# A hybrid attention block on one core: the mixer's PSUM banks as own tiles in two pools, one weight load set ahead of a reload, filler units placed in other steps

## The chip, the cores and the metric

The kernel runs on one core of a Trainium2 chip. Its engines each have a queue of instructions that they take in order: TensorE (PE, with its weight loads shown apart as PEld), VectorE (DVE), ScalarE (ACT), GpSimd (POOL) and SyncE (SP), which here issues most transfers. The metric is the device time of one execution in microseconds (us). Lower is better.

## What is computed

One layer on h, which is 16 meta tokens followed by 1024 frames of width 1024, all in float32:

```
h = h + 0.5 * swiglu(rmsnorm(h, ffn1_norm), ffn1_w_gate, ffn1_w_up, ffn1_w_down)
u = rmsnorm(h, mix_norm)
aq, ak, av, gq, gk, gv, gr, g_low, gate_a, gate_b = split(u @ w_in)
ya = window_sink_attention(aq, ak, av, att_sinks)          # 8 heads, 2 of keys, window of 3 chunks of 64
log_a = log_sigmoid(g_low @ gla_gate_w + gla_gate_b) / 16
og = gated_linear_attention(gq, gk, gv, log_a)             # S = diag(a) S + k v, o = q S, 4 heads
yb = rmsnorm(og, gla_out_norm) * silu(gr)
mixed = sigmoid(gate_a) * (ya @ w_branch_att) + sigmoid(gate_b) * (yb @ w_branch_gla)
h = h + mixed @ w_out
h = h + 0.5 * swiglu(rmsnorm(h, ffn2_norm), ffn2_w_gate, ffn2_w_up, ffn2_w_down)
return rmsnorm(h, final_norm)[16:]
```

The feed-forward width is 2816.

## The kernel before

**Precision.** Every float32 product is made as three matmuls of rounded operands: high by high, high by low part, low part by high (`mm`, L100 to L105). ACT makes the high part with a copy, DVE the low part with a subtraction (`split` L107, `Weights.cut` L127 for plain weights, `halves` L235 and L236 for the weights called `wop`).

**Order of the work.** FFN1 runs until some 702 us. Its last two feed-forward tiles are done in a loop over two halves of the tokens `c` and eight row blocks `m` (until some 727 us; `pd` is the accumulator there). That loop also starts the normalisation of the mixer's input: `tot` are the token sums of squares of a half, `rep` spreads the scales over rows, and the results are the operands `uh` and `ul`. Then come the projections for keys and queries of the linear attention (`together`, tile `pj`), the low-rank part (`low_rank`), and from 792 to 965 us the *gates stage*: 2048 columns of `w_in` in eight groups, `m` from 0 to 14 in steps of 2. A group is a seven-product scheme for a product of two-by-two blocks: seven products `i` of 12 matmuls of 128x512 each, into three accumulators `pb`, `pa` and `pd`. Product 0, 2, 4 and 6 go to `pb`, 1 to `pa`, 3 and 5 to `pd`. After each product the evacuation `gate_evac` reads the bank: ACT at L1025 copies it to a block `x`, or DVE at L1030 adds it. Weights are made two products ahead (`AHEAD = 2`), and the sums of the next group's weights (`follow.sums`, L443) are made on DVE in the last products of a group. From `m = 8` on generators called `decay` run beside the products: each begins with a matmul into a bank `z` (L1043), which ACT reads at L1044 and DVE at L1045 (writing `b`), and goes on in later products on ACT and DVE. PE, ACT and DVE follow the order of the code in this stage.

After the gates come the projections of attention's keys (AK), values (AV) and first queries (Q0), first one chunk of 512 tokens of each, then the rest (`firsts`). Columns 512 to 1023 of four `uh` and four `ul` tiles were lent to the gates stage and are loaded back from `b12_dram` with 8 loads of 128x512 (L1117), ahead of them. Then attention runs in 16 steps with one list of projection units in each (`slots`): for a step, PE makes the scores of the next one (`sp`), the units, the products with values (`po`, L1331), and the transposes of the next probabilities (`tp`, L1315, of `p`, which DVE writes at L1300). The linear attention (GLA) follows in two passes `p` of eight steps `j`. Sixteen `branch_att` units (`br`, 12 matmuls, weights `w_branch_att`, then a product with a gate `ga` on DVE at L1382, whose gate was loaded at L1378) fill places: one in each of attention's last two steps, four ahead of GLA, four in its pass 0, two in its pass 1, four behind it. GLA's inputs, 12 loads of 128x1024 with two small ones (L1424, L1426), and the gate loads share SP's queue.

**PSUM.** There are eight banks of 512 columns. FFN1 holds them as four tiles of 1024 columns, tags q0 to q3, in one pool. When its last loop ends, `dbl["open"]` is set, and `bank()` hands out the halves of such a double tile one after the other. Who may write a tile is tracked by the scheduler per tile. After the gates stage the pool is closed and a pool of eight single banks is opened (L1121 to L1123).

Of the kernel before, what the change touches and what calls it, by code (L numbers as in the profile page):

```python
# [8 lines left out]
F32 = mybir.dt.float32  # L9
# [6 lines left out]
PSUM = bass.MemoryType.PSUM  # L16

P = 128
# [17 lines left out]
def hybrid_kernel(  # L36
# [4 lines left out]
    nc = tc.nc  # L41
# [4 lines left out]
    psp = ps_singles.enter_context(tc.tile_pool(name="psp", bufs=8, space=PSUM))  # L46
# [3 lines left out]

    dbl, spare = {}, []

    def bank(name="ps"):
        if not dbl.get("open"):
            return psp.tile([P, 512], F32, tag="ps", name=name)
        if not spare:
            both = double(name)
            spare.extend([both[:, 512:], both[:, 0:512]])
        return spare.pop()

# [405 lines left out]
    N1 = T // 2  # L466
# [6 lines left out]
    nc.gpsimd.memset(shift1, 0.0)  # L473
    s_pool = f1.enter_context(tc.tile_pool(name="sums1", bufs=4))

    def acc1(kind, which, turn):

        if dbl["down"]:
            at = 2 * ((turn + (kind != "b")) % 2) + which
        else:  # L480
            at = {"b": 0 if turn % 2 == 0 else 3, "a": 1, "d": 2}[kind]
        return dbl["pool"].tile([P, 1024], F32, tag=f"q{at}", name=f"p{kind}")

# [112 lines left out]
    dgs = {}  # L596
# [162 lines left out]
    ps_singles.close()  # L759
    doubles = ExitStack()  # L760
    dbl.update(down=False, pool=doubles.enter_context(tc.tile_pool(name="psd", bufs=1, space=PSUM)))
    ffn1.gate_ups(range(2, NF - LAST))
# [16 lines left out]
    turns = [0]  # L779

    def double(name):
        turns[0] += 1
        return dbl["pool"].tile([P, 1024], F32, tag=f"q{(turns[0] - 1) % 4}", name=name)

# [39 lines left out]
    dgs = {}  # L824
    sq2 = [x[:, N1:] for x in sqs]

    def add_square(c, m):
        nc.vector.tensor_add(accs[c], accs[c], sqs[m % 3][:, 0:N1] if c == 0 else sq2[m - 1])

    for c in range(2):  # L830
        if c:
            more_sqs = [ffn1.operand(True, "sq2", F32) for _ in range(2)]
            sq2 += [x[:, i * N1:(i + 1) * N1] for x in more_sqs for i in range(2)]
        for m in range(KT):
            acc = Acc(double("pd"), N1)
            n = 0
            for f in range(LAST):
                x, w = mids[LAST * c + f], [y[:, m * P:(m + 1) * P] for y in ws[f]]
# [10 lines left out]
            if c == 0:  # L849
                if m:  # L850
                    add_square(0, m)
                if m in (1, 3):
                    hw[m // 2] = ktiles(wt.cut(raws[m // 2], eng=nc.gpsimd))
            else:
                if m < 2:
                    raws.append(wt.raw(plain_views[2 + m]))
                if m == 2:
                    dgs[0] = scales_of_half(0, double("tot"))
                if m == 4:
                    ps = double("rep")  # L860
                    scales_to_rows(0, (ps, ps[:, 512:]), dgs[0])
                if m > 4:
                    scaled(m - 5, 0)
    dbl["open"] = True

# [11 lines left out]
    b12_dram = dram.tile([4, 2, P, 512], F32, name="b12_dram")  # L877
# [117 lines left out]
    def halves_of(m, c):  # L995
        return u_hi[m][:, c * 512:(c + 1) * 512], u_lo[m][:, c * 512:(c + 1) * 512]
# [117 lines left out]
    manual.__exit__(None, None, None)  # L1114
    for k in range(4):
        for i, x in enumerate(halves_of(k, 1)):
            nc.sync.dma_start(out=x.bitcast(F32), in_=b12_dram[k, i])  # L1117
    g7.close()
    r1.close()
    wt.ws = [w_main]  # L1120
    dbl["open"] = False  # L1121
    doubles.close()
    psp = ctx.enter_context(tc.tile_pool(name="psp", bufs=8, space=PSUM))  # L1123

# [101 lines left out]
    for units in firsts:  # L1226
        units.pop(0)()
    for units in firsts:
        for u in units:
            u()  # L1230
# [161 lines left out]

    slots += [[fill.pop(0)], [fill.pop(0)]]
    values(0)
# [382 lines left out]
```

## Time and profile before

| | us |
|---|---|
| median of three runs | 2059.71 |
| lowest, highest run | 2055.99, 2059.76 |
| the profiled execution, and its span | 2057.24, 2055.5 |
| PE busy | 2006.4 (98% of the span) |
| DVE, ACT, POOL busy | 1403.1, 882.2, 178.4 |
| gates stage with the step out of it, 787 to 966 us: PE busy | 167.16 of 179 |

The page of the profile gives sums for the whole span, and the views behind it (waits, timeline, windows, the chain that ended last) give single instructions. `[2.40 <-DVE b L1045]` behind an instruction means that its engine idled 2.40 us ahead of it, and that the instruction at L1045 that wrote `b` released it. A matmul's row has its whole time through the array, while matmuls that follow each other start closer together than that.

### The profile page before, as it was taken

What the parts mean: (1) busy time and instruction counts of PE and PEld (TensorE: products, weight loads), DVE (VectorE), ACT (ScalarE), POOL (GpSimd) and SP (SyncE); (2) the same over time, 40 slices, a digit from 0 to 9 for tenths busy, and PEclk for the clock granted to TensorE, in tenths of its full rate; (3) what the DMA queues carried; (4) which work ended last, traced back from release to release, by engine and by line L of the source; (5) the groups of instructions that cost most, each with busy time, mean ns of one, the idle gap of its engine ahead of it and who ended that gap; (6) DMA issues with size and microseconds to landing.
All of it is one profiled execution on the core that took longest, in us unless ns stands there. A gap on an engine that the chain in (4) does not pass through costs nothing.

```text
span 2055.5 us, 32054 instructions
## 1 busy us (share of the span) xinstructions
PE 2006.4 (98%) x12084; PEld 1776.6 (86%) x12084; DVE 1403.1 (68%) x2441; ACT 882.2 (43%) x1722; POOL 178.4 (9%) x205
## 2 busy tenths in 40 slices
PE   8899999999999999989999999999999999999998
PEld 7899999999999987777788777888888888878888
DVE  5866677676678785465367658568876866757885
ACT  5534444444322354464256635344544544442222
POOL 1000000001323000002200000120000000022212
PEclk9999999999999999999999999999999999999999
DMA  6333344349975333354312455841543543699822
GB/s 205 106 114 125 125 168 155 125 154 343 359 283 202 101 131 99 103 163 148 79 44 66 164 182 179 262 143 44 183 156 130 179 149 125 206 371 351 278 92 83
DMA packets 285772, 343.06 MB, mean 167 GB/s; under 512 B 26406, under 2 KB 192032, under 8 KB 285616
## 3 DMA queue, kind: packets, MB, share of 16 engines
q1 hardware_dynamic: 267968, 279.60, 41.2%
q10 hardware_dynamic: 17296, 61.29, 8.0%
q8 instruction: 95, 1.56, 0.3%
q14 instruction: 61, 0.50, 0.1%
q0 software_dynamic: 352, 0.11, 0.1%
HBM read 220.66 MB, written 120.27 MB: 166 GB/s over the span
## 4 chain that ended last, share of the span: by engine, by line
PE 86%; DMA 5%; DVE 4%; ACT 3%; issue 1%; SPq 0%; DVEq 0%; ACTq 0%; POOLq 0%
PE pb L460 32%; PE pd L460 17%; PE pa L460 9%; PE pj L103 2%; PE pj L104 2%; PE pj L105 2%; PE wo L103 1%; PE wo L104 1%; PE wo L105 1%; PE br L103 1%; DMA raw<-in_ffn_w_down 1%; PE br L105 1%; PE br L104 1%; PE pd L841 1%; DMA f1mid<-kh 1%
## 5 line engine op out<-in xcount | busy, mean ns | idle before, releaser
L460 PE MATMUL pb<-tt,wop 128*128 128x260 f32 (+1 forms) x2112 | 361.1, 324 | 1.6 <-DVE x L1030 1.6
L460 PEld LDWEIGHTS pb<-tt,wop 128*128 128x128 f32 x2112 | 312.7, 188 | 34.2 <-DVE x L1030 2.4
L236 DVE TENSOR_TENSOR wop<-s,wop 128x512 fp32r<-128x512 f32 x264 | 188.1, 714 | 121.7 <-ACT wop L235 121.2
L235 ACT CAST wop<-s 128x512 fp32r<-128x512 f32 x264 | 163.7, 621 | 236.7 <-PE pb L460 90.0
L460 PE MATMUL pb<-tm,wop 128*128 128x260 f32 (+1 forms) x1440 | 237.5, 321 | 5.9 <-DVE h L347 3.5
L460 PEld LDWEIGHTS pb<-tm,wop 128*128 128x128 f32 x1440 | 209.7, 190 | 26.1 <-DVE h L347 3.9
L235 ACT CAST wop<-raw 128x512 fp32r<-128x512 f32 x198 | 122.9, 621 | 220.5 <-PE pb L460 108.4
L236 DVE TENSOR_TENSOR wop<-raw,wop 128x512 fp32r<-128x512 f32 x198 | 141.1, 715 | 30.7 <-ACT wop L235 30.4
L460 PE MATMUL pd<-tt,wop 128*128 128x260 f32 (+1 forms) x816 | 146.4, 332 | 0.0
L460 PEld LDWEIGHTS pd<-tt,wop 128*128 128x128 f32 x816 | 124.9, 188 | 15.0
L443 POOL TENSOR_TENSOR s<-raw 128x512 f32<-128x512 f32 x28 | 37.6, 1342 | 1057.5 <-DMA tm<-f1mid 453.5
L347 DVE SCALAR_TENSOR_TENSOR h<-pb,h 128x520 f32<-128x520 f32 (+1 forms) x136 | 93.8, 692 | 39.5 <-PE pb L460 37.5
L460 PE MATMUL pd<-tm,wop 128*128 128x260 f32 (+1 forms) x720 | 118.8, 319 | 0.0
L460 PE MATMUL pb<-tb,wop 128*128 128x260 f32 (+1 forms) x672 | 112.3, 320 | 0.5 <-ACT vec L94 0.5
L460 PEld LDWEIGHTS pd<-tm,wop 128*128 128x128 f32 x720 | 104.3, 188 | 9.4
L460 PE MATMUL pd<-tb,wop 128*128 128x260 f32 (+1 forms) x672 | 112.2, 320 | 0.0
L460 PE MATMUL pa<-tb,wop 128*128 128x260 f32 (+1 forms) x672 | 112.0, 320 | 0.0
L460 PEld LDWEIGHTS pb<-tb,wop 128*128 128x128 f32 x672 | 97.9, 188 | 10.0 <-ACT vec L94 0.6
L460 PEld LDWEIGHTS pd<-tb,wop 128*128 128x128 f32 x672 | 97.9, 188 | 9.4
L460 PEld LDWEIGHTS pa<-tb,wop 128*128 128x128 f32 x672 | 97.8, 188 | 9.4
L443 DVE TENSOR_TENSOR s<-raw 128x512 f32<-128x512 f32 x90 | 61.9, 688 | 56.6 <-DMA raw<-in_ffn_w_up 54.9
L103 PE MATMUL pj<-uh,whi 128*128 128x512 f32 (+2 forms) x256 | 93.1, 364 | 5.4 <-ACT whi L132 4.4
(435 smaller groups left out, 4040.6 us busy)
## 6 DMA issues: line engine op xcount, KB each, us to landing
tm<-f1mid ACTq DMA_DIRECT2D x56, 520.0 KB, 6.4
tm<-f2mid ACTq DMA_DIRECT2D x56, 512.0 KB, 5.7
raw<-in_ffn_w_gate SPq DMA_DIRECT2D x42, 512.0 KB, 3.9
raw<-in_ffn_w_up SPq DMA_DIRECT2D x42, 512.0 KB, 4.0
raw<-in_ffn_w_down SPq DMA_DIRECT2D x80, 256.0 KB, 5.5
f1mid<-kh SPq DMA_DIRECT2D x70, 260.0 KB, 3.0
f1mid<-kl SPq DMA_DIRECT2D x70, 260.0 KB, 2.9
f2mid<-kh SPq DMA_DIRECT2D x70, 256.0 KB, 2.8
```

The source lines that it names most:

```text
L103: nc.tensor.matmul(ps, wh[k], xh[k], start=(k == 0), stop=False)
L104: nc.tensor.matmul(ps, wh[k], xl[k], start=False, stop=False)
L105: nc.tensor.matmul(ps, wl[k], xh[k], start=False, stop=(k == n - 1))
L235: nc.scalar.copy(x[:, 0:n], src)
L236: nc.vector.tensor_sub(x[:, n:2 * n], src, x[:, 0:n].bitcast(F32))
L347: nc.vector.scalar_tensor_tensor(hm, ps, 0.5, hm, op0=ALU.mult, op1=ALU.add)
L443: (eng.tensor_add if add else eng.tensor_sub)(a[s], a[x], a[y])
L460: nc.tensor.matmul(ps, y, z[:, s0:s0 + sn], start=(first and k == 0 and at == 0), stop=(at == 2 and k == len(cols) - 1), skip_group_check= ...
L841: nc.tensor.matmul(ps, y, x[:, c0 + s0:c0 + s0 + sn], start=(n == 0), stop=(n == 3 * LAST - 1), skip_group_check=True)
```

## The change

Three edits, with no arithmetic added or left out.

1. **PSUM.** FFN1's four doubles lie in two pools of two. The first is closed in its last loop at `(c, m) = (1, 6)`, the second behind that loop, and each gives way to a pool of four single banks. `bank()` hands out single tiles from then on, two from the one pool and two from the other in turn. The accumulators of the last loop, `tot` and `rep` get fixed places. No pool is closed at the end of the gates stage.
2. **The reload.** The 8 loads from `b12_dram` are issued behind the first unit of AK, AV and Q0, not ahead of them.
3. **Filler units.** Attention's last two steps get two `branch_att` units each, not one. By the loops of GLA, which are as they were, this leaves four ahead of GLA, four in pass 0, none in pass 1, and four behind it.

```diff
     def bank(name="ps"):
-        if not dbl.get("open"):
-            return psp.tile([P, 512], F32, tag="ps", name=name)
-        if not spare:
-            both = double(name)
-            spare.extend([both[:, 512:], both[:, 0:512]])
-        return spare.pop()
+        return psp.tile([P, 512], F32, tag="ps", name=name)
...
+    def two_banks(at, name):
+        return dbl["pools"][at // 2].tile([P, 1024], F32, tag=f"q{at}", name=name)
...
-    doubles = ExitStack()
-    dbl.update(down=False, pool=doubles.enter_context(tc.tile_pool(name="psd", bufs=1, space=PSUM)))
+    dbl.update(down=False, a=ExitStack(), b=ExitStack())
+    dbl["pools"] = [dbl[x].enter_context(tc.tile_pool(name=f"psd{x}", bufs=1, space=PSUM, side=side))
+                    for x, side in (("a", "right"), ("b", "left"))]
...
-    def double(name):
+    def double(name, at=None):
         turns[0] += 1
-        return dbl["pool"].tile([P, 1024], F32, tag=f"q{(turns[0] - 1) % 4}", name=name)
+        return two_banks((turns[0] - 1) % 4 if at is None else at, name)
...
+    PLACES, singles, bank_turn = (0, 1, 2, 3, 0, 1, 2, 3), [], [0]
     for c in range(2):
...
         for m in range(KT):
-            acc = Acc(double("pd"), N1)
+            if (c, m) == (1, 6):
+                dbl["a"].close()
+                singles.append(ctx.enter_context(tc.tile_pool(name="psa", bufs=4, space=PSUM, side="right")))
+            acc = Acc(double("pd", m % 4 if c == 0 else PLACES[m]), N1)
...
                 if m == 2:
-                    dgs[0] = scales_of_half(0, double("tot"))
+                    dgs[0] = scales_of_half(0, double("tot", 2))
                 if m == 4:
-                    ps = double("rep")
+                    ps = double("rep", 3)
...
-    dbl["open"] = True
+    dbl["b"].close()
+    singles.append(ctx.enter_context(tc.tile_pool(name="psb", bufs=4, space=PSUM)))
+
+    def bank(name="ps"):
+        bank_turn[0] += 1
+        return singles[(bank_turn[0] - 1) // 2 % 2].tile([P, 512], F32, tag="ps", name=name)
...
-    for k in range(4):
-        for i, x in enumerate(halves_of(k, 1)):
-            nc.sync.dma_start(out=x.bitcast(F32), in_=b12_dram[k, i])
     g7.close()
     r1.close()
     wt.ws = [w_main]
-    dbl["open"] = False
-    doubles.close()
-    psp = ctx.enter_context(tc.tile_pool(name="psp", bufs=8, space=PSUM))
...
     for units in firsts:
         units.pop(0)()
+    for k in range(4):
+        for i, x in enumerate(halves_of(k, 1)):
+            nc.sync.dma_start(out=x.bitcast(F32), in_=b12_dram[k, i])
     for units in firsts:
...
-    slots += [[fill.pop(0)], [fill.pop(0)]]
+    slots += [[fill.pop(0), fill.pop(0)] for _ in range(2)]
```

**PE in the gates stage**, where product 0 of group `m = 10` ends (`pb`), the two matmuls into `z` stand, and product 1 begins. Before (each name is that of the double tile, given by whoever took its first half):

```order
L460 MATMUL pb<-uh_8387,wop 128x512
L460 MATMUL pb<-ul_8395,wop 128x512
L460 MATMUL pb<-uh_8387,wop 128x512
L1043 MATMUL pb<-glow,gw 128x512 [waits Activation_49]
L1043 MATMUL z<-glow,gw 128x16
L460 MATMUL z<-uh_8388,wop 128x512 [waits DVE_49]
L460 MATMUL z<-ul_8396,wop 128x512
```

and in the changed kernel, where L453 is the L460 of before, L1051 its L1043, and uh_8391 its uh_8388:

```order
L453 MATMUL pb<-uh_8390,wop 128x512
L453 MATMUL pb<-ul_8398,wop 128x512
L453 MATMUL pb<-uh_8390,wop 128x512
L1051 MATMUL z<-glow,gw 128x512
L1051 MATMUL z<-glow,gw 128x16
L453 MATMUL pa<-uh_8391,wop 128x512 [waits Activation_49]
L453 MATMUL pa<-ul_8399,wop 128x512
L453 MATMUL pa<-uh_8391,wop 128x512 [waits DVE_49]
```

`[waits ...]` names the engines, or the queues of transfers, whose signal an instruction waits for. The order is the same. The first `z` matmul waits for nothing, and product 1 waits with its first matmul for ACT alone (its weights' high part) and with its third for DVE (their low part), where it waited for DVE ahead of all.

**SP behind the gates stage.** Q0's weights are two loads `raw<-in_w_in 128x8x64`. Before:

```order
L124 DMA raw<-in_w_in 128x8x64 [waits DMAHW5_49,DVE_49]
L1117 DMA uh_8384<-b_dram 128x512 [waits DMAHW6_49,PE_49]
...
L1073 DMA km_dram<-k 128x512 [waits DMAHW5_49,DVE_49]
L1117 DMA ul_8392<-b_dram 128x512 [waits DMAHW6_49]
...
L1117 DMA ul_8395<-b_dram 128x512 [waits DMAHW4_49]
L124 DMA raw<-in_w_in 128x8x64 [waits DMAHW5_49]
```

and in the changed kernel:

```order
L117 DMA raw<-in_w_in 128x8x64 [waits DMAHW5_49,DVE_49]
L117 DMA raw<-in_w_in 128x8x64 [waits DMAHW6_49]
L1027 DMA gates<-x 128x512 [waits DMAHW7_49,DVE_49]
...
L1081 DMA km_dram<-k 128x512 [waits DMAHW5_49,DVE_49]
L1232 DMA uh_8387<-b_dram 128x512 [waits DMAHW6_49,PE_49]
...
L1232 DMA ul_8398<-b_dram 128x512 [waits DMAHW5_49]
```

Q0's second load passes seven stores and the eight reloads, and the first reload passes the seven stores to the other side.

**DVE in attention's last two steps**, from the maxima of the last scores to the low parts `ptl` that step 14's or 15's `po` matmuls read. Before:

```order
L1295 TENSOR_SCALAR mx<-mx 128x4 [waits DVE_49]
L1382 TENSOR_TENSOR ga<-br,ga 128x512 [waits DMAHW6_49,DMAHW7_49,DMAHW4_49,PE_49]
L1298 RECIPROCAL sm<-sm 128x4 [waits Activation_49]
L1300 TENSOR_SCALAR p<-p,sm 128x210 [waits DVE_49]
L1300 TENSOR_SCALAR p<-p,sm 128x210 x3
L1341 TENSOR_TENSOR u<-po,qs_10599 64x256 [waits PE_49,Activation_49]
L1341 TENSOR_TENSOR u<-po,qs_10599 64x256
L109 TENSOR_TENSOR ptl<-tp,pth 82x512 [waits Activation_49]
```

and in the changed kernel:

```order
L1300 TENSOR_SCALAR mx<-mx 128x4 [waits DVE_49]
L1387 TENSOR_TENSOR ga<-br,ga 128x512 [waits DMAHW6_49,DMAHW7_49,DMAHW4_49,PE_49]
L1303 RECIPROCAL sm<-sm 128x4 [waits Activation_49]
L1305 TENSOR_SCALAR p<-p,sm 128x210 [waits DVE_49]
L1305 TENSOR_SCALAR p<-p,sm 128x210 x3
L1387 TENSOR_TENSOR ga<-br,ga 128x512 [waits DMAHW5_49,DMAHW7_49,DMAHW0_49,PE_49]
L1346 TENSOR_TENSOR u<-po,qs_10622 64x256 [waits DMAHW3_49,DMAHW5_49,PE_49,Activation_49]
L1346 TENSOR_TENSOR u<-po,qs_10622 64x256
L102 TENSOR_TENSOR ptl<-tp,pth 82x512 [waits Activation_49]
```

A second product with a gate stands ahead of `u` and `ptl`, and it waits for a load.

## Rows read from the trace of the kernel before

**Rows 1.** From the page: the span, and busy time of each engine with its share of the span.

```profile
span 2055.5 us, 32054 instructions
PE 2006.4 (98%) x12084; PEld 1776.6 (86%) x12084; DVE 1403.1 (68%) x2441; ACT 882.2 (43%) x1722; POOL 178.4 (9%) x205
```

**Rows 2.** The waits of PE over the whole span: who waited for whom, us in total, how often, the longest.

```profile
PE pj L103 <- ACT whi L132: 4.4, 1, 4.4
PE z L460 <- DVE b L1045: 4.1, 2, 2.4
...
PE tp L1315 <- DVE p L1300: 3.5, 3, 2.7
...
PE z L1043 <- DVE b L1045: 2.5, 1, 2.5
...
PE pb L460 <- DVE x L1030: 1.6, 2, 0.8
PE pb L460 <- ACT x L1025: 1.4, 2, 0.7
PE pb L1043 <- ACT x L1025: 1.4, 2, 0.7
...
PE pj L103 <- DVE x L1030: 1.0, 1, 1.0
...
PE pj L924 <- ACT sums L806: 0.5, 1, 0.5
```

**Rows 3.** The timeline of PE in the gates stage: start, us, instruction, and in brackets the idle time ahead of it with its releaser. The first row is product 1 of group 0, the second product 1 of group 12.

```profile
797.75 0.50 PE L460 MATMUL pb<-uh,wop 128*128 128x512 f32 x1 [0.68 <-ACT x L1025]
...
922.81 0.73 PE L460 MATMUL z<-uh,wop 128*128 128x512 f32 x1 [2.40 <-DVE b L1045]
```

**Rows 4.** The chain that ended last, in the gates stage: start, us, what. Each row is one product of 12 matmuls.

```profile
903.50 2.73 PE pb L460 x12
...
922.81 4.61 PE z L460 x12
...
946.74 4.44 PE pa L460 x12
```

**Rows 5.** The timeline of DVE ahead of the second row of Rows 3.

```profile
917.08 0.68 DVE L236 TENSOR_TENSOR wop<-raw,wop 128x512 fp32r<-128x512 f32 x1
...
921.41 0.68 DVE L236 TENSOR_TENSOR wop<-s,wop 128x512 fp32r<-128x512 f32 x1
922.01 0.74 DVE L1045 TENSOR_SCALAR b<-z,vec 128x512 f32<-128x512 f32 x1
```

**Rows 6.** Windows: stretch, its length, busy time (and instructions) of PE, PEld, DVE, ACT and POOL, the mean clock granted to PE, the busy share of the DMA engines, and GB/s. The first row is the gates stage.

```profile
787.00:966.00 179.00, 167.16 (x721) 132.88 (x720) 96.47 (x166) 93.41 (x160) 4.22 (x12) 0.98 0.39 120
...
910.00:920.00 10.00, 9.93 (x44) 7.91 (x43) 9.69 (x22) 6.35 (x11) 0.00 (x0) 1.00 0.52 165
920.00:930.00 10.00, 7.60 (x26) 5.75 (x25) 4.65 (x8) 2.72 (x5) 0.00 (x0) 0.83 0.56 182
...
980.00:990.00 10.00, 8.32 (x28) 6.96 (x29) 1.57 (x1) 1.05 (x1) 8.78 (x20) 0.66 0.41 82
```

**Rows 7.** The timeline of SP's queue of transfers behind the gates stage. The rows at L124 are Q0's two loads (the second begins a run of three issues), the row at L1073 the last of the stores, the row at L1117 the last reload.

```profile
963.96 0.38 SPq L124 DMA_DIRECT2D raw<-in_w_in  x1
...
969.79 0.40 SPq L1073 DMA_DIRECT2D km_dram<-k  x1
...
973.34 0.42 SPq L1117 DMA_DIRECT2D ul<-b_dram  x1
973.81 5.27 SPq L124 DMA_DIRECT2D raw<-in_w_in  x3
```

**Rows 8.** The chain that ended last, behind the gates stage: Q0's second load, and single matmuls of Q0's first unit, the first one behind the wait, the last but one at the slower rate, and one behind it. Between the first two, eleven matmuls of 512 columns and seven of 256 stand in all.

```profile
973.81 6.74 DMA raw<-in_w_in
...
981.67 0.79 PE pj L103
...
987.38 0.43 PE pj L103
...
988.54 0.23 PE pj L104
```

**Rows 9.** The view of transfers: what, by which queue, how often, KB each, median us from issue to landing.

```profile
uh<-b_dram SPq DMA_DIRECT2D x4, 256.0 KB, 4.7
```

**Rows 10.** The timeline of DVE in attention's last steps, products with a gate (`ga`, idle time ahead in brackets).

```profile
1174.13 0.69 DVE L1382 TENSOR_TENSOR ga<-br,ga 128x512 f32<-128x512 f32 x1
...
1190.08 1.29 DVE L1382 TENSOR_TENSOR ga<-br,ga 128x512 f32<-128x512 f32 x2 [5.62 <-DMA ga<-gates]
```

**Rows 11.** Windows, with the columns of Rows 6, of attention's last steps.

```profile
1160.00:1170.00 10.00, 10.00 (x63) 8.53 (x62) 6.40 (x21) 6.62 (x19) 0.00 (x0) 1.00 0.72 237
...
1181.00:1192.00 11.00, 11.00 (x52) 9.17 (x51) 2.99 (x6) 1.47 (x4) 1.16 (x7) 1.00 0.83 263
```

**Rows 12.** Windows, with the columns of Rows 6, of GLA's pass 1.

```profile
1220.00:1230.00 10.00, 10.00 (x71) 7.30 (x71) 7.58 (x21) 4.08 (x15) 0.00 (x0) 1.00 0.51 170
1230.00:1240.00 10.00, 10.00 (x74) 7.17 (x72) 6.98 (x21) 6.33 (x18) 0.00 (x0) 1.00 0.23 79
1240.00:1247.00 7.00, 6.59 (x52) 4.67 (x49) 5.70 (x19) 3.80 (x19) 0.00 (x0) 1.00 0.33 112
```

**Rows 13.** Windows, with the columns of Rows 6, of the start of the mixer's projections.

```profile
727.00:740.00 13.00, 12.94 (x58) 10.18 (x57) 13.00 (x27) 7.54 (x18) 0.00 (x0) 1.00 0.18 59
```

More of the change, by code (lines that the diff above doesn't have):

```diff
@@ L49, in hybrid_kernel @@
     r_main = ctx.enter_context(tc.tile_pool(name="rmain", bufs=2))
-    dbl, spare = {}, []
     def bank(name="ps"):
-        if not dbl.get("open"):
-            return psp.tile([P, 512], F32, tag="ps", name=name)
-        if not spare:
-            both = double(name)
-            spare.extend([both[:, 512:], both[:, 0:512]])
-        return spare.pop()
+        return psp.tile([P, 512], F32, tag="ps", name=name)
     TP = 1088
@@ L474, in hybrid_kernel @@
     s_pool = f1.enter_context(tc.tile_pool(name="sums1", bufs=4))
+    dbl = {}
+    def two_banks(at, name):
+        return dbl["pools"][at // 2].tile([P, 1024], F32, tag=f"q{at}", name=name)
     def acc1(kind, which, turn):
@@ L481, in acc1 @@
             at = {"b": 0 if turn % 2 == 0 else 3, "a": 1, "d": 2}[kind]
-        return dbl["pool"].tile([P, 1024], F32, tag=f"q{at}", name=f"p{kind}")
+        return two_banks(at, f"p{kind}")
     ffn1 = Seven("f1", N1, acc1, (t_a, t_b, blk, s_pool, w_ext), ffn1_w_gate, ffn1_w_up, ffn1_w_down)
```

## The prediction, made before the changed kernel ran

> **What bounds the kernel now.** I read the page first: PE is busy 2006.4 us of a span of 2055.5, so nearly all of the time is matmuls that the change leaves as they are, and DVE with 68% has room on average [rows 1]. What can be won is PE's idle time, 49.1 us, and stretches in which its clock is low. So the list of PE's waits came next, to see which of them the edits touch: waits in the gates stage for `b` (L1045) and `x` (L1025, L1030), one for Q0's weights, one for `tp`, one for `sums` [rows 2]. The stage windows then show where the idle time sits: PE is busy 167.16 of 179 us in the gates stage, while DVE has only 96.47 there [rows 6]. A stage in which no engine is full and PE still stands waits for order, not for throughput.
>
> The timeline says which order. Product 1 of group 0 goes to `pa`, and waits 0.68 us for the ACT copy of product 0, which is in `pb` [rows 3]. Nothing computed by that copy enters product 1. The two accumulators are halves of one double tile, and the wait is the tile's, not the bank's. It is worst where a `z` shares a double tile with an accumulator: product 1 of group 12 waits 2.40 us for `b` [rows 3], and `b` is late since DVE did the next group's sums and other steps between 917.08 and 922.01, in a window in which it was busy 9.69 of 10 us [rows 5, 6].
>
> **The gates stage.** With own tiles these waits have no object: the order of the changed kernel gives `z` no wait and product 1 its two weight waits alone. Removed are 4.1 + 2.5 us for `b`, 1.6 + 1.4 for `x` ahead of products, and 1.4 for `x` ahead of `z` [rows 2]: 11.0 by rounded rows, and 10.8 by the unrounded waits that they sum. I take 10.8.
>
> A second term is the clock. Behind the two longest waits a product of 12 matmuls takes 4.61 and 4.44 us, where 2.73 is usual [rows 4], and the granted clock is 0.83 in the window of the first [rows 6]. That is a stretch at the lower of the two levels, 1.2 GHz in place of 2.4. It goes with the waits: (4.61 - 2.73) + (4.44 - 2.73) = 3.6 us. The page "TensorE: Matmul & The Clock Gate" of the Trainium skill (section on why this matters for your kernels) warns only of idle gaps longer than either of these two. By it the 3.6 us would have another cause and stay, and the forecast would stand 3.6 us higher; the rows show the low clock right behind 2.40 us of idling, and the rows decide.
>
> What is late next? The weights. PE then asks for product 1's weights at some 920.4 in place of 922.81. They were made on DVE by 917.76; those of product 2 are made by 922.1, ahead of the `b` that no longer matters to PE [rows 5], and product 2 would start at about 923.1. The slack is 1.0 us there, so the feed can cost between 0 and the whole of the three long waits and their clock (rival A). I take 0.4 us. Term: **-14.0**.
>
> **Out of the gates.** Closing the pool costs 1.0 us: AK's first matmul waits for the last `x` [rows 2]. Single tiles that stay open need no close, so it goes. Then Q0: its first load is issued at 963.96, its second at 973.81, behind the eight reloads and the stores between them, and lands 6.74 us later [rows 7, 8]. PE idles 4.4 us for its high part [rows 2], and then runs at the lower level: a matmul of 128x512 takes 0.43 us at 987.38 and 0.23 at 988.54, with a clock of 0.66 in the window [rows 8, 6]. From 981.67 to 987.8 it ran so, 6.1 us of which half is lost, 3.0. In the change both loads are issued at about 964.4 and land, by the same 6.74, near 971. PE reaches Q0 two units behind the stage's end at 965, each of 24 matmuls x 0.23 = 5.5 us: at 976. The waits and the low clock go: 1.0 + 4.4 + 3.0 = **-8.4**.
>
> The eight reloads are moved past these units in the program, but in SP's queue seven of the eight stood behind the stores already, of which the last was issued at 969.79; the last reload went at 973.34 [rows 7]. A reload lands 4.7 us after issue [rows 9], so at about 978; the second chunks need them from 965 + 3 x 5.5 = 981.5. The cover is 3.5 us, and if it fails, rival B follows. I count it at nothing.
>
> **Attention's end.** The second unit in step 14 puts 12 matmuls, 2.7 us, between the scores of step 15 and its `tp`, which waited 2.7 us for `p` [rows 2]. That wait is filled: **-2.4**, a few tenths left. The second unit's product with a gate stands on DVE ahead of `u` and `ptl`. Such products waited for their loads between nothing and 5.62 us, at 1190.08 [rows 10], while PE idled none of it [rows 11]. Now `po` of step 15 is queued behind `ptl`; two units of 2.7 us on PE cover it. Between 0 and 5.6, nearest to the row at 1174.13 that did not wait: **+0.5**.
>
> **GLA.** Pass 1 loses two units of 2.7 us. DVE's work in it is 7.58 + 6.98 + 5.70 = 20.3 us [rows 12], units' evacuations included, against 27 - 5.4 = 21.6 us of PE work left: DVE nearly level. The part of the pass without units lost 7.00 - 6.59 = 0.4 us in 7 [rows 12]; over 21.6 us that is 1.3. Bounds 0 and 5.4 (the whole cover): **+1.5**.
>
> **The mixer's start.** `tot` now stands one block of the last FFN1 loop later: 12 matmuls of 260 columns, 2.73 x 260 / 512 = 1.4 us. DVE is busy 13.00 of 13 us just behind, where PE takes its `ul` one by one [rows 13], so part of the delay shows at the end: between 0 and 1.4, **+1.0** since DVE has no slack. The wait for `sums`, where `rep` shared a double tile with `pj`, goes: **-0.5** [rows 2].
>
> Sum: -14.0 - 8.4 - 2.4 + 0.5 + 1.5 + 1.0 - 0.5 = **-22.3**. The profiled execution took 2057.24, which gives 2034.9. The median of the three runs, 2059.71, is 2.5 above that execution, and from it the sum is 2037.4. I forecast 2036, between the two.
>
> **The rivals.**
> A. *The weights take the place of the banks.* In groups 10 to 14 PE still waits behind DVE, now for `wop`. For it: 9.69 of 10 us busy on DVE [rows 6] and a slack of one microsecond. Against it: the order `wop`, then `b` [rows 5], and a mean of 96.47 in 179. Price: the three waits, 2.5 + 4.1, and the clock, 3.6: 10.2, so 2046.
>
> B. *The reloads come late.* Each waits for PE in the order, which might mean the end of the first three units, not of the last gates product. PE would then stand at the second chunks as it stood at Q0, 4.4 + 3.0, so 2043. Against it: AK's first unit ran in the kernel before ahead of the reloads' landing though it stood behind them in the program, so parts of these tiles are tracked apart.
>
> C. *DVE is held by a gate load, and the kernel is slower than before.* In steps 14 and 15 the gate loads share SP's queue with GLA's 12 inputs of 128x1024, 6.3 MB. If a gate that DVE waits for ahead of `ptl` lands behind all of them, at 237 GB/s [rows 11] that is 26.5 us, and then 3.0 of low clock as at Q0: 29.5, so 2065. It makes the kernel slower once some 28 us of it are exposed, nearly all of the queue. Against it: 5.62 us is the longest such wait, with PE busy 11.00 of 11 [rows 10, 11].
>
> D. *The change does not do what it says*: the single tiles are taken in an order that brings the same waits back, within 0.2% of 2059.7. Against it: the rows of the order. The page "PSUM — Partial Sum Buffer" of the Trainium skill (on bank collisions) asks for guarding by bank and quarter of the partitions, by which a neighbouring bank needs no wait; the trace shows one of 0.68 us between two banks, so it came from the tile.
>
> **How the numbers follow.** Forecast 0.72, A 0.10, B 0.08, C 0.05, D 0.05. The low end is the sum with its losses at their lower bounds, -22.3 - 0.4 - 0.5 - 1.5 - 1.0 = -25.7, from the profiled execution 2031.5, less 3 for other small waits and the scatter of runs: 2028. The high end takes in A and B: 2047. Outside are C and D. Some 0.2% is what a measurement of this kernel can tell from no change. Faster: forecast, A and B, 0.90; same: D, 0.05; slower: C, 0.05.
>
> **What would show it.** In the gates stage, no wait of PE for `b` or `x`, all products at 2.7 us, and PE busy beyond 0.98 of the stage. No wait for Q0's `whi`, and a clock near 1 behind the stage. `tp` of step 15 waiting under 0.5 us. Some 1 to 2 us of new waits in GLA's pass 1 for `attb` or `st`, and about 1 near 730 us. Wrong would be: waits for `wop` of 1 us and more in groups 10 to 14, a wait at the second chunks for a reload, or a stall of PE at `po` of step 15.

## The result, and the profile after

| | before | changed |
|---|---|---|
| median, us | 2057.85 (4 runs) | 2032.48 (4 runs) |
| lowest, highest | 2054.92, 2059.76 | 2029.48, 2035.58 |
| ratio of the runs | | 0.9878, 95% interval 0.9856 to 0.9901 |
| profiled execution, span | 2057.24, 2055.5 | 2034.17, 2032.5 |

The change takes 25.4 us off the median and 23.0 off the profiled span; the sum said 22.3. The page of the changed kernel answers to [rows 1]: 23 us less of span, and 7.4 less of busy time for the same matmuls, in part since the clock was lower for less of the time (mean granted clock 0.992 before, 0.995 now).

```profile
span 2032.5 us, 32056 instructions
...
PE 1999.0 (98%) x12084; PEld 1776.5 (87%) x12084; DVE 1400.4 (69%) x2441; ACT 882.1 (43%) x1722; POOL 178.2 (9%) x205
```

The waits of PE over the whole span (who waits for whom, us in total, times, the longest) answer to [rows 2]. Every wait there for `b`, `x`, `whi` and `sums` is gone, and the longest for `p` too. The list of the changed kernel has new, shorter ones: for `qs`, `o` and `ga`. The first row is FFN1's.

```profile
PE pg L631 <- ACT a L648: 7.1, 1, 7.1
...
PE br L96 <- ACT qs L1342: 1.2, 1, 1.2
...
PE tp L1320 <- DVE p L1305: 0.8, 2, 0.6
...
PE br L97 <- DVE qs L1347: 0.7, 1, 0.7
PE ot L1528 <- DVE o L1516: 0.7, 1, 0.7
PE go L1493 <- DVE ga L1387: 0.5, 1, 0.5
...
PE go L1493 <- DVE attb L1487: 0.5, 1, 0.5
```

The windows, with the columns of [rows 6], show the gates stage and what is now the first part of the projections behind it: PE busy 178.86 of 179 us at a clock of 1.00.

```profile
787.00:966.00 179.00, 178.86 (x804) 146.26 (x803) 102.90 (x176) 97.06 (x165) 16.27 (x41) 1.00 0.48 149
```

SP's timeline answers to [rows 7]. Both loads for Q0 are issued in a row at 950.41 (x2), and the eight reloads follow from 956.30 to 959.79.

```profile
950.41 1.01 SPq L117 DMA_DIRECT2D raw<-in_w_in  x2
956.30 0.45 SPq L1232 DMA_DIRECT2D uh<-b_dram  x1
...
959.79 0.42 SPq L1232 DMA_DIRECT2D ul<-b_dram  x1
```

To see where 23 us went I cut both profiles at the first matmuls of certain tiles. The view of one tile gives them, here `pj` in the changed kernel: times of one matmul, then first and last start.

```profile
L96 PE MATMUL pj<-uh,whi x256: 278/389/501, 951.5 to 1144.3; 128*128 128x512 f32 x80, 128*128 128x256 f32 x24, 128*128 128x272 f32 x24
...
L953 PE MATMUL pj<-uh,w x24: 276/287/398, 789.6 to 796.8; 128*32 128x512 f32 x8, 128*32 128x256 f32 x8, 128*32 128x272 f32 x8
```

So the gates stage with the low-rank part runs from 789.6 to 951.5, 161.9 us. The stretches of all profiles, in us:

| kernel | FFN1 to the last loop | that loop | projections | low-rank, gates | AK to first scores | attention | first filler unit to `wo` | `wo` | FFN2 |
|---|---|---|---|---|---|---|---|---|---|
| before | 702.4 | 24.9 | 58.9 | 180.0 | 63.1 | 140.8 | 133.5 | 88.4 | 663.5 |
| before, second profile | 702.2 | 24.9 | 59.0 | 179.9 | 61.6 | 140.8 | 135.0 | 88.5 | 663.3 |
| changed | 705.8 | 26.2 | 57.6 | 161.9 | 55.5 | 140.7 | 135.2 | 88.4 | 661.2 |
| changed, second profile | 702.4 | 26.1 | 57.6 | 161.9 | 55.6 | 140.6 | 134.8 | 88.4 | 660.9 |
| banks_alone | 701.5 | 26.1 | 57.6 | 161.9 | 57.3 | 140.7 | 135.0 | 88.4 | 661.5 |
| reload_first | 706.4 | 26.1 | 57.6 | 161.9 | 57.3 | 140.7 | 135.0 | 88.5 | 661.8 |
| one_unit_per_step | 702.1 | 26.1 | 57.7 | 161.8 | 55.6 | 140.7 | 135.7 | 88.5 | 661.3 |
| old_banks_reload_late | 704.6 | 24.9 | 58.9 | 181.3 | 55.6 | 140.7 | 133.4 | 88.4 | 661.3 |
| sums_early | 702.5 | 24.9 | 58.9 | 180.5 | 61.8 | 140.7 | 134.0 | 88.4 | 661.7 |
| two_then_one | 705.3 | 26.2 | 57.6 | 161.9 | 55.5 | 140.7 | 133.5 | 88.5 | 661.2 |
| two_ahead_of_gla | 702.6 | 26.1 | 57.7 | 161.9 | 55.5 | 140.8 | 133.1 | 88.4 | 662.0 |
| first_half_units | 703.1 | 26.1 | 57.6 | 161.9 | 55.5 | 140.7 | 134.2 | 88.4 | 661.4 |
| fillers_mended | 703.2 | 26.2 | 57.6 | 161.9 | 55.6 | 140.7 | 134.9 | 88.5 | 661.4 |
| closed_together | 701.9 | 26.1 | 57.6 | 162.0 | 55.5 | 140.7 | 139.5 | 88.5 | 661.1 |

Stretches that an edit does not touch mostly repeat to 0.2 us from kernel to kernel, and tell apart what runs that scatter by 5 us can't. FFN1, whose order of work no edit changes, scatters between 701.5 and 706.4: 705.8 and 702.4 are one and the same kernel. Where PE waits, the second profile of the kernel before differs from the first by 1.5 us in two stretches, so a difference from the kernel before is given by both.

### The profile page after: what moved, and what is told of

Same layout as the page of the kernel before. It is cut to its first block, busy times and chain, and to the rows that moved or that the text cites. A ratio compares the mean times of both kernels' runs of the same rounds, so it can differ in the third digit from the quotient of the medians.

```text
span 2032.5 us, 32056 instructions
## 1 busy us (share of the span) xinstructions
PE 1999.0 (98%) x12084; PEld 1776.5 (87%) x12084; DVE 1400.4 (69%) x2441; ACT 882.1 (43%) x1722; POOL 178.2 (9%) x205
## 5 line engine op out<-in xcount | busy, mean ns | idle before, releaser
L453 PE MATMUL pb<-tt,wop 128*128 128x260 f32 (+1 forms) x2208 | 383.9, 327 | 0.0
L453 PEld LDWEIGHTS pb<-tt,wop 128*128 128x128 f32 x2208 | 330.9, 188 | 35.5
L453 PE MATMUL pb<-tm,wop 128*128 128x260 f32 (+1 forms) x1440 | 235.9, 320 | 5.5 <-DVE h L340 3.3
L453 PEld LDWEIGHTS pb<-tm,wop 128*128 128x128 f32 x1440 | 208.6, 190 | 25.1 <-DVE h L340 3.7
L453 PE MATMUL pd<-tt,wop 128*128 128x260 f32 (+1 forms) x768 | 135.1, 329 | 0.0
L453 PEld LDWEIGHTS pd<-tt,wop 128*128 128x128 f32 x768 | 115.9, 188 | 13.1
L453 PE MATMUL pd<-tm,wop 128*128 128x260 f32 (+1 forms) x720 | 118.8, 319 | 0.0
L453 PE MATMUL pb<-tb,wop 128*128 128x260 f32 (+1 forms) x672 | 112.3, 320 | 0.5 <-ACT vec L87 0.5
L453 PEld LDWEIGHTS pd<-tm,wop 128*128 128x128 f32 x720 | 104.3, 188 | 9.3
L453 PE MATMUL pd<-tb,wop 128*128 128x260 f32 (+1 forms) x672 | 112.2, 320 | 0.0
L453 PE MATMUL pa<-tb,wop 128*128 128x260 f32 (+1 forms) x672 | 112.0, 320 | 0.0
L453 PEld LDWEIGHTS pb<-tb,wop 128*128 128x128 f32 x672 | 97.9, 188 | 9.9 <-ACT vec L87 0.6
L453 PEld LDWEIGHTS pd<-tb,wop 128*128 128x128 f32 x672 | 97.9, 188 | 9.3
L453 PEld LDWEIGHTS pa<-tb,wop 128*128 128x128 f32 x672 | 97.8, 188 | 9.3
L340 DVE SCALAR_TENSOR_TENSOR h<-pd,h 128x520 f32<-128x520 f32 (+3 forms) x112 | 72.7, 655 | 33.3 <-PE pd L453 17.5
```

What stands on the lines that cost most here:

```text
L340: nc.vector.scalar_tensor_tensor(hm, ps, 0.5, hm, op0=ALU.mult, op1=ALU.add)
L453: nc.tensor.matmul(ps, y, z[:, s0:s0 + sn], start=(first and k == 0 and at == 0), stop=(at == 2 and k == len(cols) - 1), skip_group_check= ...
```

## Experiments: the three edits apart

**The changed kernel again**, beside the next three on one chip.

> The changed kernel once more, as the reference for the three partial kernels that run beside it on the same chip. Theory 1 (own tiles in the gates stage and the order of Q0's loads carry the gain, the filler units carry none of it): 1.2% below the kernel before, some 2033 us beside 2058. From the start of the low-rank part to AK's first matmul some 162 us beside 180, from there to the first scores 55.5 beside 63.1, from the first filler unit to the first w_out matmul 135.2 beside 133.5. Rival (part of the gain is scatter of FFN1 and FFN2, whose code is the same): the gain shrinks to some 20 us or less.

2032.75 us, ratio 0.9881 (0.9867 to 0.9895). The gain is not scatter.

**The third edit undone.**

```diff
-    slots += [[fill.pop(0), fill.pop(0)] for _ in range(2)]
+    slots += [[fill.pop(0)], [fill.pop(0)]]
```

> The changed kernel with the third edit undone: one filler unit in each of attention's last two steps, so two in GLA's pass 1 again. Theory 1 (the filler units fill the wait of 2.7 us for p, but bring waits for the last attention output, for gate loads and in pass 1 that cost more): 1 to 2 us faster than the changed kernel, some 2031; from the first filler unit to the first w_out matmul 133.5 us, the wait of tp back at 2.7 us, the waits for qs gone, and those of pass 1 near 0.4. Rival (the prediction's sum: filler units gain 0.4 on balance): 0.4 us slower than the changed kernel.

2030.83 us, ratio 0.987 (0.9857 to 0.9884), inside the changed kernel's interval. The stretch took 135.7 us where I expected 133.5: wrong. The wait for `p` is back at its old length, in PE's timeline:

```profile
1150.64 1.56 PE L1320 MATMUL tp<-ident,p 128*82 128x128 f32 x8 [2.69 <-DVE p L1305]
```

But here a low clock came behind it, which the window of this kernel shows (mean clock 0.86), and the first profile of the kernel before did not have:

```profile
1144.00:1154.00 10.00, 7.31 (x35) 6.09 (x34) 7.94 (x25) 5.53 (x17) 0.00 (x0) 0.86 1.01 357
```

So the stretch of the kernel before is 133.5 or, with the low clock, 135.0, as in its second profile. Beside that, the third edit changes the stretch by between -0.9 and +1.7 us, by which profile it is held against. In sum it can't be told from nothing.

**The second edit undone.**

```diff
+    for k in range(4):
+        for i, x in enumerate(halves_of(k, 1)):
+            nc.sync.dma_start(out=x.bitcast(F32), in_=b12_dram[k, i])
     g7.close()
...
     for units in firsts:
         units.pop(0)()
-    for k in range(4):
-        for i, x in enumerate(halves_of(k, 1)):
-            nc.sync.dma_start(out=x.bitcast(F32), in_=b12_dram[k, i])
```

> The changed kernel with the second edit undone: the eight reloads from b12_dram ahead of the first units. Theory 1 (Q0's second load stands behind the stores and reloads in SP's queue): PE waits 4 to 5 us for Q0's whi again and runs at the lower clock behind it, AK's first matmul to the first scores 63 us, some 7 us slower than the changed kernel, 2040. Rival (the wait came from the pool that was closed, not from the queue): no wait, same time as the changed kernel.

2038.35 us, ratio 0.9913 (0.9896 to 0.9929). The median is 5.6 us above the changed kernel, near what I expected, but not for my reason. AK to the first scores took 57.3 us, 1.8 longer and not 7.5, and PE has no wait for `whi`. The rest of the difference to `changed_again`'s profile lies in FFN1 (706.4 beside 702.4) and FFN2 (661.8 beside 660.9), where the order of work is the same. `banks_alone` below, with the same order of loads but one filler unit per step, has the lower median again. So 1.8 us is what the second edit is worth beside the new banks, by the stretch; why this kernel's four runs lay higher is open.

**The second edit alone, on the kernel before.**

```diff
-    for k in range(4):
-        for i, x in enumerate(halves_of(k, 1)):
-            nc.sync.dma_start(out=x.bitcast(F32), in_=b12_dram[k, i])
     g7.close()
...
     for units in firsts:
         units.pop(0)()
+    for k in range(4):
+        for i, x in enumerate(halves_of(k, 1)):
+            nc.sync.dma_start(out=x.bitcast(F32), in_=b12_dram[k, i])
```

> The kernel before with the second edit alone: reloads behind the first units, banks as halves of double tiles, one filler unit per step. Theory 1 (edits add up): some 7.5 us faster than the kernel before, 2050; the gates stage as in the kernel before, with the waits for b and x and the low clock behind two of them. Rival (with the old banks the pool's close holds the queue as well, so that the order of loads alone gains little): under 3 us faster.

2050.85 us, ratio 0.9972 (0.996 to 0.9984). As expected: 55.6 us from AK to the first scores, 7.5 less than in the first profile of the kernel before and 6.0 less than in the second, and the waits for `b` and `x` as before. The order of Q0's loads is worth 6.0 to 7.5 us beside the old banks and 1.8 beside the new.

**The first edit alone**, formed from that difference (both edits above undone in the changed kernel).

> The first edit alone: own banks in two pools, with the reloads ahead of the first units and one filler unit per step. Theory 2 (formed from the runs so far: with the banks free the scheduler itself puts second chunks of AK and AV ahead of Q0's first unit, and the late load costs 2 us in place of 7.5): gates stage 161.9 us, AK to the first scores 57.3, first filler unit to w_out 133.5 to 135.7, about 2034, so that the banks carry 22 or more of the 24.5 us. Theory 1 in its first form (the edits' parts add up as in the prediction, 14 and 8): AK to the first scores 63, about 2040.

2032.58 us, ratio 0.9874 (0.9857 to 0.9892): the banks alone give all of the gain that the medians can tell; the stretches leave 1.8 us to the second edit. Theory 2 stands, my first theory's sum of parts falls. Q0's `whi` is as late as ever in this kernel, cast on ACT behind a wait of 5.98 us for the load:

```profile
961.86 1.05 ACT L125 CAST whi<-raw 128x1024 fp32r<-128x1024 f32 x1 [5.98 <-DMA raw<-in_w_in]
```

but PE is not at Q0 then. The scheduler put AK's last chunk (24 matmuls of 128x272) ahead of Q0's first unit, and PE waits only for single reloads in it:

```profile
959.21 0.39 PE L97 MATMUL pj<-ul,whi 128*128 128x272 f32 x1 [0.16 <-DMA ul<-b_dram]
...
960.67 0.39 PE L97 MATMUL pj<-ul,whi 128*128 128x272 f32 x1 [0.40 <-DMA ul<-b_dram]
```

The order of PE's units (tile, weights, columns, matmuls) says the same. Before:

```
pj_10766 whi_10762 128x512 2 | pj_10795 whi_10692 128x256 7 | pj_10766 wlo_10763 128x512 22
```

where whi_10762 is Q0's, taken up behind AK's and AV's first units. With own banks and the old order of loads, whi_10793 being Q0's:

```
pj_10857 whi_10723 128x272 24 | pj_10894 whi_10760 128x256 3 | pj_10797 whi_10793 128x512 2
```

**When the first pool is closed.**

```diff
-            if (c, m) == (1, 6):
-                dbl["a"].close()
-                singles.append(ctx.enter_context(tc.tile_pool(name="psa", bufs=4, space=PSUM, side="right")))
...
+    dbl["a"].close()
+    singles.append(ctx.enter_context(tc.tile_pool(name="psa", bufs=4, space=PSUM, side="right")))
     dbl["b"].close()
```

> The changed kernel with the first pool of doubles closed behind the last FFN1 loop, with the second, and not two row blocks ahead of its end. Theory (the gain is from the banks being own tiles, not from the time of the close; the four banks of the first pool are read long before the first projection): the stretch from the loop to the low-rank part 83.8 us as in the changed kernel, within half a us, gates stage 161.9, time the same. Rival (the early close is what lets PE run into the projections without a wait, and the tile tracking then holds PE for the last pd): 1 us or more of waits of PE near 730 us and a longer time by as much.

2034.28 us, ratio 0.9882 (0.9866 to 0.9899): the same, and the same 26.1, 57.6 and 162.0 us in the stretches that it touches. The early close of the first pool is not what gains. That there are two pools was not tried apart.

## Experiments: the waits and the clock behind them

**The sums one product earlier in DVE's queue**, on the kernel before.

```diff
-                if j == 8:
+                if j == 7:
                     follow.sums(nc.vector)
```

> The kernel before with one line moved: the four sums of the next group's weights stand one product earlier in DVE's queue, so ahead of the product whose bank shares a tile with z by one product more. No bank and no work changes. Theory 1 (the long waits for b are DVE's queue ahead of b, and the low clock is caused by the length of these waits): the two waits of 2.4 us for b shrink to about 0.8, the clock stays at 1 in the gates stage, and the stage from the low-rank part to AK loses 2 x 1.6 + 3.6, some 7 us of its 180; the waits of 0.7 and 0.8 us for x stay. Rival (DVE is short of throughput in these groups): the waits move to another product or to the weights, and the stage gains under 2 us.

2058.49 us, ratio 1.0001 (0.9991 to 1.0012): no gain, and the rival was nearer. PE's waits from 780 to 1035 us in this kernel:

```profile
PE pj L103 <- ACT whi L132: 4.2, 1, 4.2
PE z L460 <- DVE b L1045: 3.5, 2, 1.8
PE pd L460 <- ACT wop L235: 2.4, 2, 1.2
PE z L1043 <- DVE b L1045: 1.8, 1, 1.8
PE pb L460 <- ACT x L1025: 1.7, 2, 1.0
...
PE pd L460 <- DVE x L1030: 0.9, 2, 0.5
```

The waits for `b` shrank to 1.8 us and not to 0.8, since DVE, now ready earlier, waits ahead of `b` for ACT's reading of the same `z`:

```profile
925.02 0.75 DVE L1045 TENSOR_SCALAR b<-z,vec 128x512 f32<-128x512 f32 x1 [0.67 <-ACT e L1044]
```

and new waits came for weights (2.4) and for a late evacuation (0.9). The clock stayed at 1.00 from 880 to 970 us, and the product behind the wait took 3.01 us, not 4.61:

```profile
925.83 3.01 PE z L460 x12
```

So the low clock is a cost of its own, which can go without the wait. The stage took 180.5 us all the same: the new waits took what the clock gave back. This order on DVE does not remove the waits; other orders were not tried.

**The kernel before, a second profile.**

> The kernel before once more, for a second profile of it. Theory (the low clock behind waits of 1.7 to 2.7 us comes behind some of them and not others, from run to run): the same waits as in the first profile to a tenth of a us, but other products among those behind them take 4 us and more, and the gates stage differs from 180.0 by a us or two. Rival (the low clock is fixed by the length of the wait): the same two products as in the first profile.

The chain of this profile has the low clock behind the same two waits, at 922.64 and 946.55, within 0.2 us of the times in [rows 4], and 3.01 us behind a wait of 1.7:

```profile
900.31 3.01 PE z L460 x12
...
922.64 4.61 PE z L460 x12
...
946.55 4.44 PE pa L460 x12
```

That speaks for the rival. But in `old_banks_reload_late`, where this stage begins 2.2 us later and the waits are as long, the chain reads otherwise:

```profile
902.68 5.49 PE z L460 x12
...
927.93 4.31 PE z L460 x12
...
951.88 2.84 PE pa L460 x12
```

The low clock came behind the wait of 1.7 us, and not behind one of 2.45. So neither stands: the length of a wait alone does not decide, and yet the two profiles of one kernel, 0.2 us apart in this stage, have it behind the same waits. The wait for `p` (2.69 to 2.70 us in all three) had no low clock behind it in the first profile, and a clock of 0.83 in the second:

```profile
1170.00:1180.00 10.00, 7.31 (x34) 5.87 (x33) 6.80 (x23) 4.34 (x14) 0.00 (x0) 0.83 0.96 369
```

Q0's wait differs too: 4.0 us with a clock of 0.83 behind it, beside 4.4 and 0.66 in the first profile [rows 2, 6], and AK to the first scores took 61.6 us beside 63.1:

```profile
980.00:990.00 10.00, 8.83 (x38) 7.55 (x39) 1.24 (x2) 1.63 (x2) 8.81 (x21) 0.83 0.38 73
```

## Experiments: the filler units

In the changed kernel, DVE's timeline behind attention shows what the second units brought. Two products with a gate wait 4.08 and 0.72 us for their loads, ahead of `u` and the last `qs`:

```profile
1162.57 0.69 DVE L1387 TENSOR_TENSOR ga<-br,ga 128x512 f32<-128x512 f32 x1 [4.08 <-DMA ga<-gates]
1163.98 0.69 DVE L1387 TENSOR_TENSOR ga<-br,ga 128x512 f32<-128x512 f32 x1 [0.72 <-DMA ga<-gates]
```

and PE waits for `qs`, since the next units are those on tokens 512 to 1023:

```profile
1163.49 1.20 PE L96 MATMUL br<-qs,whi 128*128 128x512 f32 x4 [1.22 <-ACT qs L1342]
1166.26 0.50 PE L97 MATMUL br<-qs,whi 128*128 128x512 f32 x1 [0.70 <-DVE qs L1347]
```

In pass 1 DVE is nearly full (9.03 of 10) and PE waits for it:

```profile
1210.00:1220.00 10.00, 8.84 (x72) 6.51 (x74) 9.03 (x26) 4.79 (x16) 0.00 (x0) 1.00 0.16 52
```

**One unit given back.**

```diff
-    slots += [[fill.pop(0), fill.pop(0)] for _ in range(2)]
+    slots += [[fill.pop(0), fill.pop(0)], [fill.pop(0)]]
```

> The changed kernel with two filler units in attention's step 14 and one in step 15; one unit comes back to GLA's pass 1. Theory 1 (the second unit of step 14 fills the wait for p; what costs are the waits for qs and the missing units in pass 1): the wait of tp stays near nothing and some of the loss goes: from the first filler unit to the first w_out matmul 133.5 us or less, 1 to 2 us faster than the changed kernel. Rival (any unit taken from GLA is lost there): as the changed kernel, 135.

2033.52 us, ratio 0.9878 (0.9864 to 0.9893); the stretch 133.5 us, 1.3 to 1.7 less than in the changed kernel. As expected by the stretch; the median doesn't show it.

**Two units ahead of GLA, two in pass 1.**

```diff
-    for _ in range(4):
+    for _ in range(2):
         fill.pop(0)()
     for p in range(2):
```

> The changed kernel with two filler units ahead of GLA in place of four, so that pass 1 has its two again. Theory 1: the waits of pass 1 (o, attb, 1.5 us) go, those for qs and the gate (1.9 and 0.5) stay, since the first unit behind attention still needs its last output: 133.5 to 134.5 us in that stretch. Rival (the loss is all in the waits for qs): 135 as in the changed kernel.

2029.94 us, ratio 0.986 (0.9845 to 0.9875), the stretch 133.1 us. The waits of pass 1 went, one of those for `qs` stayed:

```profile
PE br L96 <- ACT qs L1342: 1.2, 1, 1.2
PE go L1493 <- DVE a L1529: 0.8, 1, 0.8
...
```

From the first filler unit to the first `br` product that reads GLA's output it took 88.6 us, beside 90.5 in the changed kernel. Not all of these 1.9 us are pass 1's. From the first state product of pass 1 to that `br` product it is 32.1 us in the changed kernel, and 36.3 here with two more units of 2.72: 1.2 us are what the units missing in pass 1 cost. The other 0.7 lie ahead of it, where the second wait for `qs` (0.7) and the one for a gate (0.5) are gone as well.

**Units on the first half of the tokens first.**

```diff
-    fill = fill[0][0:2] + fill[1][0:2] + fill[0][2:4] + fill[1][2:4] + fill[2] + fill[3]
+    fill = fill[0][0:2] + fill[1][0:2] + fill[2][0:2] + fill[0][2:4] + fill[1][2:4] + fill[2][2:4] + fill[3]
```

> The changed kernel with the filler units in another order: the third set's two units on tokens 0 to 511 come ahead of all units on tokens 512 to 1023, so that the first two behind attention don't read its last output. Theory 1 (PE waits there for qs, which DVE writes behind two products that wait for gate loads): the waits for qs, 1.9 us, go, the waits of DVE for gate loads stay and cost PE nothing there; pass 1 as in the changed kernel: 133 us in that stretch. Rival (GLA's inputs, not qs, hold PE there): 135.

2029.4 us, ratio 0.9861 (0.9845 to 0.9876), the stretch 134.2 us. The waits for `qs` went as expected, and PE then idled 2.6 us at GLA's first state, until 1174.40:

```profile
PE kv L1478 <- issue: 2.6, 1, 2.6
```

The profile names no releaser, but DVE's timeline shows one that fits. That product reads `km`, which DVE copies at L1464, behind products with a gate that wait for their loads, and the copy ends 0.1 us ahead of it:

```profile
1171.78 1.31 DVE L1387 TENSOR_TENSOR ga<-br,ga 128x512 f32<-128x512 f32 x2 [0.61 <-DMA ga<-gates]
1173.42 0.69 DVE L1387 TENSOR_TENSOR ga<-br,ga 128x512 f32<-128x512 f32 x1 [0.33 <-DMA ga<-gates]
1174.03 0.27 DVE L1464 COPY km<-km 16x128 f32<-16x128 f32 x1
```

So the expectation that DVE's waits for gate loads cost PE nothing here was wrong, and GLA's inputs, the rival's cause, are not what shows: its other operand, `gvm`, shows its last landing at 1170.2 (one of its four loads shows none).

**Both together.**

> The changed kernel with both changes of the filler units together: two of them ahead of GLA in place of four, and the units on the first half of the tokens first. Theory (the missing units of pass 1 cost 1.9 us, the waits behind attention 2.2): from the first filler unit to the first w_out matmul 131 to 132.5 us beside 135, about 2029 and the fastest kernel of the study. Rival (the waits behind attention are for GLA's inputs, which PE meets as soon as the waits for qs are gone): 133, as with either change alone.

2031.64 us, ratio 0.9867 (0.9852 to 0.9882), the stretch 134.9 us, beside 131 to 132.5 and 133 expected: neither number came, but the rival's mechanism did. PE waits at the same product, now for one of GLA's small inputs, which SP issues behind the twelve large ones:

```profile
1169.10 0.54 PE L1478 MATMUL kv<-gvm,km 16*64 16x128 f32 x4 [2.49 <-DMA gvm<-gvm_dram]
```

With two units ahead of GLA and no wait for `qs`, PE reaches it before its inputs have landed. The low clock came behind this wait (mean clock 0.66 from 1169 to 1174 us), and the unit behind it took 4.54 us, 1.7 more than at the full clock; without that the stretch would be near the rival's 133. Behind the 2.58 us in `first_half_units` it did not come (1.00 from 1172 to 1182). The fastest medians of the study, 2029.4 and 2029.9, are 2.5 to 3.1 us below the changed kernel's, inside its interval.

In `closed_together` the gate loads came later still. A step of GLA waits 2.87 us for DVE, held by such a product, and the clock fell to 0.78 in the window; both make its stretch 139.5:

```profile
1182.12 0.79 PE L1492 MATMUL go<-gv,attb 128*128 128x128 f32 x2 [2.87 <-DVE ga L1386]
```

```profile
1175.00:1185.00 10.00, 7.13 (x40) 4.54 (x39) 3.82 (x10) 1.72 (x6) 0.00 (x0) 0.78 0.76 262
```

## Why the prediction held, point by point

- **Gates stage, -14.0, and the close, -1.0: right in the mechanism, sized too low.** The low-rank part and the gates took 180.0 us and now take 161.9, 18.1 less, where 15.0 was forecast. All waits went, and PE needs no more than the products' own time: no wait for weights came, so the 0.4 for the feed was not needed, and rival A is out. What the sum missed is PE's restart. A product right behind a short wait took 3.01 us and a little more in every kernel with the old banks, beside 2.73 [rows 4], so each wait costs 0.3 us beyond its idle time. With seven short waits that is 2.0 of the 3.1 us; with the 0.4 for the feed, 0.7 is left. By the starts of single matmuls, 0.3 of that lies in the low-rank part, whose matmuls stand in another order now; the rest is without a cause.
- **Q0's loads, -7.4: the size was right (-7.6 by the first profile of the kernel before, -6.1 by the second), the cause was split wrongly.** What failed is the premise that PE's order of units stays as it was unless the loads move. The 3.0 for the low clock is not fixed either: the second profile has less of it. `old_banks_reload_late` shows 6.0 to 7.5 us for the loads alone, `banks_alone` that with own banks the scheduler covers most of that with AK's last chunk. The terms overlap, and only their sum was tested by the result. Rival B did not come: the reloads land in time in the changed kernel.
- **Attention's end, GLA: -2.4 + 0.5 + 1.5 forecast, between +1.7 and -0.2 measured** by the first and the second profile of the kernel before. The wait for `p` went. The units missing in pass 1 cost 1.2, near the 1.5. The +0.5 for DVE held by a gate load was mis-sized: PE waits 1.9 us for `qs` and 0.5 for a gate in GLA's first steps, with their restarts, where I had 0.5. It is rival C's mechanism, at 2.4 of its 29.5 us; `closed_together` shows it larger.
- **The mixer's start, +1.0 - 0.5: about nothing measured.** The loop is 1.2 to 1.3 longer and the projections 1.3 shorter: the delay was taken up later.
- **FFN2, not in the sum: -2.3.** Its code is the same. In both profiles of the kernel before the mean clock was 0.98 in the window behind a wait for `h` (1.8 to 2.0 us); in the changed kernel's second profile it is 1.00 there, behind 1.2. The kernels with the old banks and one edit took 661.3 and 661.7 as well, so this is no gain of the banks. In `sums_early`, one of these, the wait is 2.0 us again, and the clock from 1800 to 1900 is 1.00. Here is the second profile of the kernel before:

```profile
1800.00:1900.00 100.00, 98.21 (x427) 80.80 (x426) 67.62 (x94) 34.91 (x60) 27.19 (x19) 0.98 0.99 363
```

- Added up from the stretches behind FFN1, the first profiles give 1.3 - 1.3 - 18.1 - 7.6 - 0.1 + 1.7 - 2.3 = -26.4, and FFN1's scatter puts +3.4 on that: -23.0, the difference of the spans. That this lies 0.7 from the -22.3 is partly luck: the stretches behind FFN1 gave 4.1 more than the sum, with misses of either sign among them, and FFN1 took 3.4 back.

Left open: why the four runs of `reload_first` lay 3 to 4 us above the others with the same stretches, and what else than a wait's length decides whether the low clock follows. A filler with more units early enough that also covers GLA's small inputs was not tried.

## What to carry to other kernels

Where one engine bounds the kernel and idles beside others that are half empty, look for tiles that hold more than one unit of work: if the scheduler tracks whole tiles, a reader of one half holds the writer of the other. Price a wait with what follows it, the restart and perhaps a low clock, and not with its idle time alone. And test edits one by one in both directions: here one edit was worth 6.0 to 7.5 us on the old kernel and 1.8 on the new, since the scheduler found another order by itself.

## What was not expected of the hardware

A short wait of PE cost 0.3 us beyond its idle time in these streams of matmuls of 512 columns (products of 3.01 beside 2.73 us). The lower clock of TensorE followed waits of 1.7 to 2.7 us in some executions and not in others of the same length: behind 1.7 us a product took 3.01 us in one kernel and 5.49 in another, behind 2.45 us 4.44 and 2.84; at GLA's first state it came behind 2.49 us and not behind 2.58. It cost 1.5 to 3 us each time. What part of the scatter of the runs it makes is not shown: the changed kernel, which has lost most of these waits, scattered by 6.1 us in four runs, the kernel before by 4.8.
